# Scores of the sliding-window heads: both groups' products ahead of both minima in their shared bank, and other buffers for the first projection's unsplit input

## The chip, the cores and the metric

The kernel runs on one core of one Trainium2 chip. The time is the device time of one execution in microseconds (us). Before the change it is 308.17 us, the median of 3 runs (307.82 to 308.65).

The core has a matrix engine (TensorE, PE in the profile; its weight loads have a row of their own, PEld), a vector engine (VectorE, DVE), an activation engine (ScalarE, ACT), a small general one (GpSimd, POOL) and one that here only issues transfers (SyncE, SP). Matrix products are accumulated in PSUM, which has banks of 512 fp32 columns for each of 128 partitions; everything else lives in SBUF.

## The reference

One decoder layer on 512 tokens of width 1024, batch 1: a modulated normalisation, one wide projection, two groups of attention heads side by side, a gate on each, an output projection.

```python
mod = jax.nn.silu(c) @ w_ada + b_ada
shift, scale, gate = jnp.split(mod, 3, axis=-1)
h = rms_norm(x, norm_gain) * (1 + scale[:, None, :]) + shift[:, None, :]
proj = h @ w_in
(q_a, k_a, v_a, z_a, q_b, kc, vc, ks, vs, kw, vw, z_b, g_b) = jnp.split(proj, _split_points(), axis=-1)
...
o_a = banded_gqa(qa, ka, heads(v_a, A_KV), SWA_WINDOW, rel_bias[:, :A_HEADS], sinks)
...
o_b = gb[..., 0, :] * o_cmp + gb[..., 1, :] * o_sel + gb[..., 2, :] * o_win
y = jnp.concatenate([o_a.reshape(Bn, S, D_A) * jax.nn.silu(z_a.astype(jnp.float32)),
                     o_b.reshape(Bn, S, D_B) * jax.nn.silu(z_b.astype(jnp.float32))], axis=-1)
out = y.astype(x.dtype) @ w_out
return x + gate[:, None, :] * out
```

Group A has 8 query heads on 2 key/value groups with a window of 128 tokens, a bias by distance and a sink for each head in the softmax. Group B has 8 query heads on 2 groups as well, with a compressed, a selected and a windowed (512) branch.

## The kernel before

**Precision and stages.** The inputs are fp32. A product of two fp32 numbers is made of three products of halves: high by high, high by low and low by high, where high is the number rounded by the engine's fp32r type and low is the rest. So the first projection's input h exists as hh (high), hl (low) and, between the two, hf (unsplit: `h_high`, L285 to L289, writes hh and hf on ScalarE; `h_low`, L291 and L292, subtracts on VectorE). The first projection (queries, keys and values of group A) is an `in_order` section up to 51 us. After it come the other projections (L503, 256 columns each; L513, 512 columns) and, from 65 us on, the attention slots between them. The output projection ends the program.

**Slots.** Attention is cut into slots of 128 queries. A slot of kind a is one query head of each of the two key/value groups (heads r and 4 + r) and one block i of four: 16 slots, from about 65 to 148 us. A slot of kind b does the same for one branch of group B, from about 157 us. `run` (in program order) deals for each step t: the transposes of slot t−2 (`slot_trans`, L971), the scaling of slot t−1 (`slot_scale`, L952 to L960), the scores of slot t (`slot_scores`, L923 to L935), a share of the projections, and after a head's last block the products with the values (`slot_pv`, L998). `block()` keeps TensorE's instructions of these pieces together in this order among each other; between them, and on the other engines, the tile scheduler sets the order from the program order and the buffers in use. A packer gives every pool its places (`auto_bufs`), so another buffer in one place can move tiles in others.

**The scores of a slot.** For each group g two matmuls (by the high and low half of the keys) form 128 by up to 512 products in PSUM; one VectorE instruction (`tensor_tensor_reduce`, L928) adds the bias, writes the sum to P in SBUF and puts the smallest into nm (signs are turned, so it is the softmax maximum). ScalarE takes the exponential (L935) and its sum. In kind a both groups write one bank, `ps_a`, 256 columns each; in kind b each has a bank of its own. The pool of these banks, ps_s, has two.

**Other names.** pt is a bank for transposes, wh and wl the halves of a projection's weights, qs a head's queries, kT the keys, first and rest small constants, gate rows (L248) are VectorE reductions that make the layer's gate from raw rows of weights and lie between group B's slots.

Of the kernel before, what the change touches and what calls it, by code (L numbers as in the profile page):

```python
# [9 lines left out]
F32 = mybir.dt.float32  # L10
# [9 lines left out]
S, D, HD, NB = 512, 1024, 64, 4  # L20
# [62 lines left out]
def hybrid_layer_kernel(ctx, tc, A, out):  # L83
    nc = tc.nc
    PE, DVE, ACT, POOL, SP = nc.tensor, nc.vector, nc.scalar, nc.gpsimd, nc.sync
# [9 lines left out]
    def T2(dt, name):  # L95
        return t2.tile([128, S], dt, name=name, tag="t2")
# [100 lines left out]
    stp = st.enter_context(tc.tile_pool(name="stp", bufs=1))  # L197
# [71 lines left out]
    hf, y, ws = {}, {}, {}  # L269
# [13 lines left out]
            DVE.tensor_tensor(y[k][:, c], xT[k][:, c], by[:, c], op=OP.mult)  # L283

    def h_high(k, parts=(slice(0, S),)):  # L285
        hf[k] = T2(F32, "hf")
        for t in (hh[k], hf[k]):
            for c in (parts if t is hh[k] else parts[:0] + (slice(0, S),)):
                ACT.activation(t[:, c], y[k][:, c], AF.Identity, bias=AB[:, k, 1:2], scale=AB[:, k, 0:1])  # L289
# [16 lines left out]
    with in_order(tc) as begun:  # L306
# [83 lines left out]
        scaled(1, rbp)  # L390
        weights_high(0)
        rb = stp.tile([128, S], F32, name="rb")
        hf[0] = T2(F32, "hf")
        for c in (quarters[0], quarters[1], halves[1]):
            ACT.activation(hh[0][:, c], y[0][:, c], AF.Identity, bias=AB[:, 0, 1:2], scale=AB[:, 0, 0:1])
        ACT.activation(rb, rbp, AF.Copy)
# [8 lines left out]
        def new_tile(k):  # L405

            if k in PE_MOD:
                mod_ab(k)
            h_high(k, halves)
            if k == 7:  # L410
                h_low(k)
                return
            weights_high(k + 1)
            mod_shift(k + 1)
            if k > 1:
                h_low(k)
            mod_scale(k + 1)
            if k == 1:
                h_low(k)
            weights_low(k + 1)  # L420
            if 1 < k < 6:
                scaled(k + 2, rb)
# [56 lines left out]
    ps_s = ctx.enter_context(tc.tile_pool(name="ps_s", bufs=2, space=PSUM))  # L479
# [46 lines left out]
    qs = {}  # L526
    kT = {}
# [360 lines left out]
    def slot_scores_both(sl, P):  # L888

        r = sl["id"][1]  # L890
        nm = sm.tile([128, 2, 2], F32, name="nm2", bufs=2)
        dn = sm.tile([128, 2, 2], F32, name="dn2", bufs=2)
        for g in range(2):
            ps = ps_s.tile([128, 512], F32, name="s")[:, 0:256].rearrange("p (b k) -> p b k", b=2)
            for hl_ in range(2):
                PE.matmul(ps, qs[8 + 4 * g + r][:, 0:128], kTb[g][:, :, hl_, 0:128], start=hl_ == 0, stop=hl_ == 1)
            for b in range(2):
                DVE.tensor_tensor_reduce(out=P[:, g, 128 * b:128 * b + 128], in0=ps[:, b], in1=bias["b", r, g][:, 384:512],
                                         scale=1.0, scalar=3e38, op0=OP.add, op1=OP.min, accum_out=nm[:, g, b:b + 1])
        for g in range(2):  # L900
            for b in range(2):
                v = P[:, g, 128 * b:128 * b + 128]
                ACT.activation(v, v, AF.Exp, bias=nm[:, g, b:b + 1], scale=-1.0, accum_out=dn[:, g, b:b + 1])
        sl.update(P=P, dn=dn, w=256, lo=0)

    def slot_scores(sl):
        kind, r, br, i = sl["id"]
        lo = max(0, i - 1) * 128 if kind == "a" else 0
        w = (i + 1) * 128 - lo
        P = mp.tile([128, 2, 257], F32, name="pa", bufs=3) if kind == "a" else mp.tile([128, 2, 512], F32, name="pp", bufs=3)  # L910
        if br == 3:
            slot_scores_both(sl, P)
            return
        nm = sm.tile([128, 2], F32, name="nm", bufs=4)
        dn = sm.tile([128, 2], F32, name="dn", bufs=4)
        ps_a = ps_s.tile([128, 512], F32, name="s") if kind == "a" else None
        for g in range(2):
            h = (0 if kind == "a" else 8) + 4 * g + r
            n = max(w, 256)
            ps = ps_a[:, 256 * g:256 * g + n] if kind == "a" else ps_s.tile([128, 512], F32, name="s")[:, 0:n]  # L920
            k = kT[br, g]
            for hl_ in range(2):
                PE.matmul(ps, qs[h][:, 128 * i:128 * i + 128], k[:, hl_, lo:lo + n], start=hl_ == 0, stop=hl_ == 1)  # L923
            if kind == "a":
                bt, init = bias["a", r][:, g, 256 - w:256], nsink[:, h:h + 1]
            else:
                bt, init = bias["b", r, g][:, 512 - w:512], 3e38
            DVE.tensor_tensor_reduce(out=P[:, g, 0:w], in0=ps[:, 0:w], in1=bt, scale=1.0, scalar=init,  # L928
                                     op0=OP.add, op1=OP.min, accum_out=nm[:, g:g + 1])
        e = w  # L930
        if kind == "a":
            POOL.tensor_copy(P[:, :, w:w + 1], nsink[:, r:8:4][:, :, None])
            e = w + 1
        for g in range(2):
            ACT.activation(P[:, g, 0:e], P[:, g, 0:e], AF.Exp, bias=nm[:, g:g + 1], scale=-1.0,  # L935
                           accum_out=dn[:, g:g + 1])
        sl.update(P=P, dn=dn, w=w, lo=lo)
# [77 lines left out]
    def run(slots, stream):  # L1015
# [3 lines left out]
        for t in range(n + 3):  # L1019
            per = PER_A if t < 16 else PER_B[t - 16 >= PER_B[2]]  # L1020
            if t < n:
                kind, r, br, i = slots[t]["id"]
                if kind == "a" and i == 0 and r >= 2:
                    load_bias_b(r - 2)
            if 0 <= t - 2 < n:
                with block():
                    slot_trans(slots[t - 2])
            if 0 <= t - 1 < n:
                slot_scale(slots[t - 1])
            if t < n:  # L1030
                with block():
                    slot_scores(slots[t])
            stream.adv(per / 2)
            if 0 <= t - 3 < n:
                group.append(slots[t - 3])
                kind, r, br, i = slots[t - 3]["id"]
                if i == NB - 1 and (kind == "a" or br == 2):
                    with block():
                        for sl in group:
                            slot_pv(sl)  # L1040
                        if jobs:
                            jobs.pop(0)()
                            stream.debt += 3.6
                    group = []
                    if kind == "b" and br == 2 and r + 2 < 4:
                        load_bias_b(r + 2)
            stream.adv(per / 2)
# [103 lines left out]
```

## Time and profile before

| what | us |
|---|---|
| median of 3 runs | 308.17 |
| the profiled execution | 307.14 |
| its span | 305.4 |
| PE busy | 298.1 (98%) |
| DVE busy | 239.0 (78%) |
| ACT busy | 196.3 (64%) |

The profile is of one execution. Its span goes from the first to the last instruction; its time has 1.74 us more around it. Busy times are of the instructions; PE and PEld overlap. A stretch's row ("64.00:85.00 21.00") gives its length and each engine's busy time in it with the number of instructions, then the clock that TensorE was granted, the share of the transfer engines and their rate. A row of the waits reads: engine and line that waited, what it waited for, us in total, times, longest. A row of the timeline reads: start, duration, engine, line, operation, out<-in, and in brackets how long the engine stood idle before it and what ended that.

### The profile page before, as it was taken

The numbers are of one execution on the slowest core, as the hardware profiler recorded it, in microseconds if no ns is written. First come the engines' busy times: TensorE is split into PE (matmuls) and PEld (weight loads), VectorE is DVE, ScalarE is ACT, GpSimd is POOL, SyncE is SP. The second block draws the span as 40 slices with busy tenths as digits, with TensorE's granted clock in tenths as the row PEclk, the third lists the DMA queues.
The fourth block names the chain that finished last, engine by engine and source line by source line (L and its number), as shares of the span: only waits on it lengthen the run. The fifth ranks groups of instructions, "written<-read, shape, count | busy, mean of one in ns | idle before, by whom it ended". The sixth has DMA issues, their size and how long they took to land.

```text
span 305.4 us, 5858 instructions
## 1 busy us (share of the span) xinstructions
PE 298.1 (98%) x2118; PEld 252.6 (83%) x2119; DVE 239.0 (78%) x669; ACT 196.3 (64%) x474; POOL 4.6 (1%) x26
## 2 busy tenths in 40 slices
PE   8899999999999999999999999999999999999995
PEld 4577888888999999999886788788888888788885
DVE  3899996999995487787899999999996985817411
ACT  4876457876885569948657756875876875823200
POOL 1000000100000000000000000000000000000000
PEclk9999999999999999999999999999999999999999
DMA  7999929897233980340542422472000000005401
GB/s 258 384 379 409 386 76 286 293 249 284 75 100 103 345 264 14 102 142 2 170 140 72 138 71 69 131 280 75 21 14 2 0 2 1 2 0 188 158 34 71
DMA packets 27420, 44.21 MB, mean 145 GB/s; under 512 B 1712, under 2 KB 19408, under 8 KB 27392
## 3 DMA queue, kind: packets, MB, share of 16 engines
q1 hardware_dynamic: 27392, 43.84, 41.9%
q8 instruction: 17, 0.28, 0.3%
q14 instruction: 11, 0.09, 0.1%
HBM read 41.70 MB, written 2.14 MB: 144 GB/s over the span
## 4 chain that ended last, share of the span: by engine, by line
PE 79%; DVE 9%; DMA 5%; ACT 3%; issue 2%; SPq 1%; DVEq 0%; ACTq 0%
PE pj L513 29%; PE s L923 8%; PE po L998 8%; PE pj L503 7%; PE sq L299 7%; PE pt L981 4%; PE pt L971 4%; PE skv L300 4%; DMA ada_ring<-in_w_ada_ss 3%; PE s L630 2%; DMA raw<-in_w_cmp 2%; DVE wl L181 2%; DVE qs L563 1%; DVE pa L928 1%; ACT pa L935 1%
## 5 line engine op out<-in xcount | busy, mean ns | idle before, releaser
L180 ACT ACTIVATE wh<-raw 128x512 fp32r<-128x512 f32 (+1 forms) x52 | 31.9, 637 | 18.1 <-PE pj L513 14.0
L181 DVE TENSOR_TENSOR wl<-raw,wh 128x512 fp32r<-128x512 f32 (+1 forms) x52 | 35.4, 689 | 9.3 <-issue 3.4
L503 PE MATMUL pj<-wl,hh 128*128 128x256 f32 (+1 forms) x128 | 36.7, 287 | 0.0
L503 PE MATMUL pj<-wh,hh 128*128 128x256 f32 (+1 forms) x128 | 36.7, 287 | 0.0
L503 PE MATMUL pj<-wh,hl 128*128 128x256 f32 (+1 forms) x128 | 36.5, 285 | 0.0
L935 ACT ACTIVATE pp<-pp,nm 128x256 f32<-128x256 f32 (+2 forms) x48 | 29.2, 610 | 8.8 <-DVE nm L928 8.7
L513 PE MATMUL pj<-hh,wh 128*128 128x512 f32 x80 | 32.3, 403 | 0.0
L513 PE MATMUL pj<-hh,wl 128*128 128x512 f32 x80 | 31.8, 398 | 0.0
L513 PE MATMUL pj<-hl,wh 128*128 128x512 f32 x80 | 31.7, 397 | 0.0
L928 DVE CUSTOM_DVE_ANT_0 pp<-s,bias 128x256 f32<-128x256 f32 (+2 forms) x48 | 25.5, 552 | 2.9 <-PE s L923 2.8
L513 PE MATMUL pj<-yl,wh 128*128 128x512 f32 (+1 forms) x72 | 26.8, 373 | 0.0
L513 PE MATMUL pj<-yh,wl 128*128 128x512 f32 (+1 forms) x72 | 26.8, 372 | 0.0
L513 PE MATMUL pj<-yh,wh 128*128 128x512 f32 (+1 forms) x72 | 26.3, 371 | 0.0
L503 PEld LDWEIGHTS pj<-wl,hh 128*128 128x128 f32 x128 | 24.1, 188 | 0.4 <-issue 0.3
L503 PEld LDWEIGHTS pj<-wh,hh 128*128 128x128 f32 x128 | 24.1, 188 | 0.2 <-issue 0.2
L503 PEld LDWEIGHTS pj<-wh,hl 128*128 128x128 f32 x128 | 24.1, 188 | 0.2 <-issue 0.2
L923 PE MATMUL s<-kTb,qs 128*128 128x256 f32 (+2 forms) x96 | 23.4, 356 | 0.0
L956 DVE TENSOR_SCALAR pp<-pp,rr,grev 128x256 f32<-128x256 f32 (+2 forms) x48 | 21.0, 476 | 0.6
L928 DVE CUSTOM_DVE_ANT_0 pa<-s,bias,nsink 128x256 f32<-128x256 f32 (+1 forms) x32 | 14.3, 449 | 4.9 <-PE s L923 3.4
L982 ACT COPY ptT<-pt 128x384 f32<-128x384 f32 (+1 forms) x32 | 15.7, 527 | 3.6 <-PE pt L981 3.6
L513 PEld LDWEIGHTS pj<-hh,wl 128*128 128x128 f32 x80 | 15.1, 189 | 3.2
L513 PEld LDWEIGHTS pj<-hl,wh 128*128 128x128 f32 x80 | 15.0, 188 | 3.1 <-issue 0.2
(246 smaller groups left out, 702.1 us busy)
## 6 DMA issues: line engine op xcount, KB each, us to landing
ada_ring<-in_w_ada_ss SPq DMA_DIRECT2D x16, 512.0 KB, 9.4
raw<-in_w_cmp SPq DMA_DIRECT2D x8, 512.0 KB, 6.0
raw<-in_w_gate SPq DMA_DIRECT2D x8, 512.0 KB, 3.3
raw<-in_w_o SPq DMA_DIRECT2D x8, 512.0 KB, 5.4
wst_ring<-in_w_qkv_a SPq DMA_DIRECT2D x8, 384.0 KB, 9.2
bias<-line_d SPq DMA_DIRECT2D x8, 256.0 KB, 3.1
xr<-in_xT SPq DMA_DIRECT2D x8, 256.0 KB, 4.1
raw<-in_w_q_b SPq DMA_DIRECT2D x4, 512.0 KB, 5.9
```

The source lines that it names most:

```text
L180: ACT.activation(wh, src, AF.Copy)
L181: DVE.tensor_tensor(wl, src, wh.bitcast(F32), op=OP.subtract)
L299: PE.matmul(pj_q[tb], lt, w[:, 0:512], start=f, stop=l, skip_group_check=True)
L300: PE.matmul(pj_kv[tb // 2][:, tb % 2, :], lt, w[:, 512:768], start=f and tb % 2 == 0, stop=l, skip_group_check=True)
L503: PE.matmul(bank[:, t * n:(t + 1) * n], h[:, tb * 128:(tb + 1) * 128], w[:, k % 2, :], start=k == 0 and m == 0, stop=k == 7 and m == 2)
L513: PE.matmul(bank, w, h[:, cols], start=k == 0 and m == 0, stop=k == 7 and m == 2)
L923: PE.matmul(ps, qs[h][:, 128 * i:128 * i + 128], k[:, hl_, lo:lo + n], start=hl_ == 0, stop=hl_ == 1)
L928: DVE.tensor_tensor_reduce(out=P[:, g, 0:w], in0=ps[:, 0:w], in1=bt, scale=1.0, scalar=init, op0=OP.add, op1=OP.min, accum_out=nm[:, g:g + 1])
L935: ACT.activation(P[:, g, 0:e], P[:, g, 0:e], AF.Exp, bias=nm[:, g:g + 1], scale=-1.0, accum_out=dn[:, g:g + 1])
L956: DVE.tensor_scalar(v, v, rr[:, g:g + 1], gates[:, g, br:br + 1], op0=OP.mult, op1=OP.mult)
L982: ACT.copy(T[:, 0:nb, :], rev(pt[:, 0:nb * 128].rearrange("p (b q) -> p b q", b=nb)))
L998: PE.matmul(o[64 * g:64 * g + 64, 128 * i:128 * i + 128], vb[:, 64 * g:64 * g + 64], sl["T"][g][:, b, :], start=first_of and b == 0, stop= ...
```

## The change

In `slot_scores` the loop over the two groups is split: first all four matmuls, then both minima. In kind a the first group's minimum stood between the two groups' products before. In kind b the code's order changes likewise, each group in its bank. The first projection's unsplit input hf is taken from the stage's pool stp (named hf, two buffers) in place of the general pool t2.

```diff
     def h_high(k, parts=(slice(0, S),)):
-        hf[k] = T2(F32, "hf")
+        hf[k] = stp.tile([128, S], F32, name="hf", bufs=2)
...
         rb = stp.tile([128, S], F32, name="rb")
-        hf[0] = T2(F32, "hf")
+        hf[0] = stp.tile([128, S], F32, name="hf", bufs=2)
...
         ps_a = ps_s.tile([128, 512], F32, name="s") if kind == "a" else None
+        ps = []
         for g in range(2):
             h = (0 if kind == "a" else 8) + 4 * g + r
             n = max(w, 256)
-            ps = ps_a[:, 256 * g:256 * g + n] if kind == "a" else ps_s.tile([128, 512], F32, name="s")[:, 0:n]
-            k = kT[br, g]
+            ps.append(ps_a[:, 256 * g:256 * g + n] if kind == "a" else ps_s.tile([128, 512], F32, name="s")[:, 0:n])
             for hl_ in range(2):
-                PE.matmul(ps, qs[h][:, 128 * i:128 * i + 128], k[:, hl_, lo:lo + n], start=hl_ == 0, stop=hl_ == 1)
+                PE.matmul(ps[g], qs[h][:, 128 * i:128 * i + 128], kT[br, g][:, hl_, lo:lo + n], start=hl_ == 0,
+                          stop=hl_ == 1)
+        for g in range(2):
+            h = (0 if kind == "a" else 8) + 4 * g + r
             if kind == "a":
                 bt, init = bias["a", r][:, g, 256 - w:256], nsink[:, h:h + 1]
             else:
                 bt, init = bias["b", r, g][:, 512 - w:512], 3e38
-            DVE.tensor_tensor_reduce(out=P[:, g, 0:w], in0=ps[:, 0:w], in1=bt, scale=1.0, scalar=init,
+            DVE.tensor_tensor_reduce(out=P[:, g, 0:w], in0=ps[g][:, 0:w], in1=bt, scale=1.0, scalar=init,
                                      op0=OP.add, op1=OP.min, accum_out=nm[:, g:g + 1])
```

From here on the lines of the changed kernel are three higher: the minimum is L931, the exponential L938, the scaling L952 to L963, the transposes L974, the products with the values L1001. The matmuls of the scores stay on L923.

The order of the instructions changes in these places. On TensorE, at slot 13 (about 135 us; kT_645 and kT_647 are the keys of the two groups, qs_921 and qs_924 the queries), before:

```order
L557 MATMUL pt<-first,qn 128x128 x3
L971 MATMUL pt<-first,pa 128x128 [waits PE_49]
L971 MATMUL pt<-first,pa 128x128 x3
L923 MATMUL s<-kT_645,qs_921 128x256 x2
L503 MATMUL pj<-wh,hh 128x256
L503 MATMUL pj<-wl,hh 128x256
L503 MATMUL pj<-wh,hl 128x256
L503 MATMUL pj<-wh,hh 128x256
L503 MATMUL pj<-wl,hh 128x256
L503 MATMUL pj<-wh,hl 128x256
L923 MATMUL s<-kT_647,qs_924 128x256 [waits DVE_49]
```

and now:

```order
L557 MATMUL pt<-first,qn 128x128 x3
L974 MATMUL pt<-first,pa 128x128 [waits PE_49]
L974 MATMUL pt<-first,pa 128x128 x3
L923 MATMUL s<-kT_645,qs_921 128x256 x2
L923 MATMUL s<-kT_647,qs_924 128x256 x2
L503 MATMUL pj<-wl,hh 128x256
L503 MATMUL pj<-wh,hl 128x256
```

The second group's products moved ahead of six projection matmuls and wait for VectorE no more. It is alike in 15 of the 16 slots of group A; in slot 0 the products stay spread out.

On TensorE, at slots 7 and 8 (about 111 us; qs_799 and qs_802 are slot 7's queries, qs_850 and qs_853 slot 8's, gsig the gates of the branches), before:

```order
L923 MATMUL s<-kT_647,qs_802 128x256 [waits DVE_49]
L923 MATMUL s<-kT_647,qs_802 128x256
L971 MATMUL pt<-first,pa 128x128 x4
L923 MATMUL s<-kT_645,qs_850 128x256 x2
L788 MATMUL pt<-gsig,rest 128x96
L503 MATMUL pj<-wh,hh 128x256
L503 MATMUL pj<-wl,hh 128x256
L503 MATMUL pj<-wh,hl 128x256
L923 MATMUL s<-kT_647,qs_853 128x256 [waits DVE_49]
```

and now:

```order
L923 MATMUL s<-kT_645,qs_799 128x256 x2
L923 MATMUL s<-kT_647,qs_802 128x256 x2
L974 MATMUL pt<-first,pa 128x128 x4
L923 MATMUL s<-kT_645,qs_850 128x256 x2
L923 MATMUL s<-kT_647,qs_853 128x256 x2
L788 MATMUL pt<-gsig,rest 128x96 [waits DVE_49]
L503 MATMUL pj<-wh,hl 128x256
```

Slot 7's first products stood six projection matmuls ahead of its second, and now stand right ahead of them; slot 8's second products moved ahead of the gate transpose and three projection matmuls. Slot 7's own transposes come after fourteen projection matmuls in the new order; before they came thirteen after slot 8's second products.

On VectorE, at the first slot of group B (about 160 us; the four L949 rows are its scalings, rr_2105 their factors), before:

```order
L945 RECIPROCAL rr_2105<-dn_2037 128x4
L181 TENSOR_TENSOR wl<-raw,wh 128x512
L861 TENSOR_TENSOR yl_2081<-yf,yh_2080 128x512
L949 TENSOR_SCALAR pp<-pp,rr_2105,grev 128x128 x2
L563 TENSOR_TENSOR qs_2092<-pt,qs_2092 64x512
L949 TENSOR_SCALAR pp<-pp,rr_2105,grev 128x128 x2
L952 RECIPROCAL rr<-dn 128x2
```

and now:

```order
L948 RECIPROCAL rr_2105<-dn_2037 128x4
L248 ISA raw,gate_lsb<-raw,scb,first 128x1024
L248 ISA gate_lsb 128x1
L563 TENSOR_TENSOR qs_2092<-pt,qs_2092 64x512
L181 TENSOR_TENSOR wl<-raw,wh 128x512
L952 TENSOR_SCALAR pp<-pp,rr_2105,grev 128x128
L563 TENSOR_TENSOR qs_2095<-pt,qs_2095 64x512
L952 TENSOR_SCALAR pp<-pp,rr_2105,grev 128x128 x3
```

The gate row, which came ten rows after the last of these scalings, now stands ahead of the first. On TensorE the four transposes of this slot stand ten projection matmuls (L513) later than before.

## The prediction

> **What bounds the kernel now.** I read the engine totals first, then the line of the scores, then the waits stage by stage. The page's first part and the row of group A's minima:
>
> ```profile
> PE 298.1 (98%) x2118; PEld 252.6 (83%) x2119; DVE 239.0 (78%) x669; ACT 196.3 (64%) x474; POOL 4.6 (1%) x26
> ...
> L928 DVE CUSTOM_DVE_ANT_0 pa<-s,bias,nsink 128x256 f32<-128x256 f32 (+1 forms) x32 | 14.3, 449 | 4.9 <-PE s L923 3.4
> ```
>
> TensorE is almost the whole span, so a microsecond in which it stands still is a microsecond of the time, unless a later wait would have stopped it anyway. The query on the scores' line shows where it stands still:
>
> ```profile
> L923 PEld LDWEIGHTS s<-kT,qs x64: 186/189/192, 65.3 to 146.9; 128*128 128x128 f32 x64
> L923 PE MATMUL s<-kT,qs x64: 277/288/388, 65.3 to 147.1; 128*128 128x256 f32 x64
> ...
> its engine sat idle before it (us, times) until:
>   DVE nm L928: 3.9, 14
> ...
> ```
>
> That wait is the second group's products waiting for the first group's minimum, because both write one bank. It is what the change removes: 3.9 us in 14 records. One of them as the timeline has it (start, duration, engine, line; the idle time before and its releaser in brackets), slot 13, TensorE's weight loads:
>
> ```profile
> 135.86 0.19 PEld L503 LDWEIGHTS pj<-wl,hh 128*128 128x128 f32 x1
> 135.98 0.19 PEld L503 LDWEIGHTS pj<-wh,hl 128*128 128x128 f32 x1
> 136.36 0.30 PEld L923 LDWEIGHTS s<-kT,qs 128*128 128x128 f32 x2 [0.19 <-DVE nm L928]
> 136.59 0.19 PEld L503 LDWEIGHTS pj<-wh,hh 128*128 128x128 f32 x1
> ```
>
> Loads follow one another every 0.12 us (135.86 to 135.98), and the one that waited came 0.38 us after its predecessor: 0.26 us lost, which is the bracket's 0.19 and 0.07 more, since a load of 0.19 us normally overlaps the next by 0.07. Per stage the waits of the weight loads are these (total, times, longest), for 64 to 85, 85 to 93, 110 to 121, 121 to 135 and 135 to 148 us in this order:
>
> ```profile
> PEld s L923 <- DVE nm L928: 0.9, 2, 0.5
> PEld s L923 <- DVE nm L928: 0.2, 1, 0.2
> PEld s L923 <- DVE nm L928: 0.6, 3, 0.2
> PEld s L923 <- DVE nm L928: 0.6, 2, 0.4
> PEld s L923 <- DVE nm L928: 0.9, 3, 0.4
> ```
>
> That is 3.2 us in 11 loads. With 0.07 us for each it is 1.04, 0.27, 0.81, 0.74 and 1.11 us: 4.0 us, the most that the change can give through these waits. What each stage lets through depends on the other engines (busy time of PE, PEld, DVE, ACT, POOL in each stretch, granted clock):
>
> ```profile
> 64.00:85.00 21.00, 20.23 (x159) 19.14 (x158) 20.08 (x46) 16.82 (x41) 0.38 (x2) 1.00 0.62 194
> ...
> 110.00:121.00 11.00, 10.98 (x100) 10.06 (x100) 8.92 (x38) 8.79 (x25) 0.77 (x4) 1.00 0.34 114
> 121.00:135.00 14.00, 13.47 (x112) 12.80 (x109) 10.72 (x33) 10.54 (x26) 0.37 (x2) 1.00 0.40 130
> 135.00:148.00 13.00, 12.92 (x111) 11.62 (x110) 9.84 (x25) 11.26 (x28) 0.38 (x2) 1.00 0.07 26
> 148.00:172.00 24.00, 24.00 (x153) 18.16 (x152) 23.36 (x65) 15.52 (x40) 0.00 (x0) 1.00 0.38 125
> ...
> 230.00:272.00 42.00, 42.00 (x383) 35.92 (x379) 28.07 (x94) 27.69 (x77) 0.00 (x0) 1.00 0.01 1
> ```
>
> **The change part by part.** No instruction of the scores is added or removed: the 64 matmuls, 32 minima and 32 exponentials stay. The sum is made against the profiled execution's own 307.14 us (its span of 305.4 and 1.74 around it); the median shown is 308.17, 1.03 more, and the difference I find is taken off that.
>
> *64 to 85 us (slots 0 to 3), 1.04 us removed.* VectorE is busy 20.08 of 21 us here, as nearly full as TensorE, and what follows the scores on TensorE is waiting for VectorE's work. Slot 1's wait and what stands around it:
>
> ```profile
> 73.01 0.48 DVE L928 CUSTOM_DVE_ANT_0 pa<-s,bias,nsink 128x256 f32<-128x256 f32 x1
> 73.42 0.28 DVE L960 TENSOR_SCALAR pa<-pa,rr 128x128 f32<-128x128 f32 x1
> 73.55 0.30 PEld L923 LDWEIGHTS s<-kT,qs 128*128 128x128 f32 x2 [0.43 <-DVE nm L928]
> 73.80 0.24 PEld L971 LDWEIGHTS pt<-first,pa 128*128 128x128 f32 x2
> ```
>
> The transposes that follow at 73.80 need the scaling that ended at 73.70 (73.42 and 0.28). Without the wait at 73.55 TensorE reaches them 0.5 us sooner and waits there for the same scaling. So this stage moves its wait and gains nothing. Bounds: 1.04 gained, or 0.3 lost if slot 0's first minimum, now behind all four products, is late by a gap of VectorE. I take 0.
>
> *85 to 93 us, 0.27 us removed.* One wait, with VectorE no longer full. I take 0.2 (0 to 0.27).
>
> *110 to 121 us (slots 7 to 10), 0.81 us removed.* Here the order of the matmuls packs tighter than the work between allows. Slot 7 in the timeline, from its second products to its transposes:
>
> ```profile
> 111.63 0.30 PEld L923 LDWEIGHTS s<-kT,qs 128*128 128x128 f32 x2 [0.19 <-DVE nm L928]
> 112.17 0.48 DVE L928 CUSTOM_DVE_ANT_0 pa<-s,bias,nsink 128x256 f32<-128x256 f32 x1
> 113.09 0.51 ACT L935 ACTIVATE pa<-pa,nm 128x257 f32<-128x257 f32 x1
> 114.71 1.01 ACT L958 ACTIVATE pa<-pa,rr 128x256 f32<-128x256 f32 x2
> 115.32 0.42 PEld L971 LDWEIGHTS pt<-first,pa 128*128 128x128 f32 x4
> ```
>
> From the second minimum's start to the transposes go 3.15 us (112.17 to 115.32). With all four products together that minimum starts about 1.1 us after the first product's load (four loads at 0.12, 0.28 for the last product and one minimum of 0.41, from 73.01 to 73.42, ahead of it, less overlaps), so the transposes can start some 4.2 us after it, or 3.8 if the later slot's minima are less in the way. By the order TensorE has eight products, four transposes, one gate transpose and fourteen projection matmuls in between: 27 at 0.12, about 3.3 us. A new wait of 0.5 to 1.0 us takes the place of the old ones. I take 0 (0.8 gained to 0.5 lost).
>
> *121 to 135 us (slots 11 and 12), 0.74 us removed.* TensorE has a wait of 0.5 us left on the normalised queries at 133.74, and slot 12's share runs into it; slot 11's does not. I take 0.5 (0 to 0.74).
>
> *135 to 148 us (slots 13 to 15), 1.11 us removed.* VectorE has over 3 us of slack in 13, and the transposes stand well behind the scores (the next load of slot 13 after the products is a projection's). I take 1.0 (0.5 to 1.11).
>
> *148 us on, group B.* Group B's two groups have always had banks of their own, so its products and minima only change their order in the code. TensorE is full here and VectorE nearly so: 23.36 of 24 us. A shift gained before 148 passes through if VectorE comes earlier too, and it stood idle waiting for TensorE's projections just before (9.84 of 13 busy). But the order on VectorE changes: a gate row (L248) stands ahead of the first group-B slot's four scalings, where it stood behind them.
>
> ```profile
> 158.83 0.72 PE L923 MATMUL s<-kTb,qs 128*128 128x256 f32 x4
> 161.73 0.59 DVE L949 TENSOR_SCALAR pp<-pp,rr,grev 128x128 f32<-128x128 f32 x2
> 163.07 0.60 DVE L949 TENSOR_SCALAR pp<-pp,rr,grev 128x128 f32<-128x128 f32 x2
> 163.47 0.33 PE L971 MATMUL pt<-first,pp 128*128 128x128 f32 x1
> 168.02 1.28 DVE L248 CUSTOM_DVE_ANT_0 raw<-raw,scb,first 128x1024 f32<-128x1024 f32 x1
> ```
>
> TensorE already waits for the second pair (released in the middle of the row at 163.07). In the new order 1.28 us of gate row and two rows of some 0.65 stand ahead of the first scaling, 2.6 us; TensorE's transposes come ten projection matmuls later, about 2.3 us by the pitch of the twelve between 158.83 and the first pair of transposes. Nearly even: I take 0.4 us lost (none to 1.3).
>
> *The unsplit input in two buffers of its own.* The eight tiles came one after the other out of the pool t2, in one place; now they have places in another pool. The only thing this frees is ScalarE's write waiting for VectorE's subtraction of the tile before. ScalarE has to wait in the same loop for the scale and shift in any case:
>
> ```profile
> ACT hh L289 <- DVE AB L255: 10.0, 5, 2.2
> ```
>
> Those 10.0 us are the cover; were they gone, ScalarE would still write at the pace of VectorE's subtraction. I take 0. The lower weights' transfers and buffers move around too, because the pools are laid out anew; the order shows no wait added for it.
>
> **Sum.** 0 + 0.2 + 0 + 0.5 + 1.0 − 0.4 = 1.3 us gained: 305.8 us for the profiled execution, **306.9 us** as a median.
>
> **Rivals.**
>
> *All of it is gained.* The slots' later consumers wait nowhere, 4.0 us and no loss in group B: 304.2 us. For it: TensorE is 98% of the span. Against it: the rows at 73.42 and 115.32, where consumers follow directly. The Trainium skill ("Perfetto Trace Analysis", Identifying the Most-Contended Engine) takes the engine of the highest occupancy as the one to work on first; by that rule every wait of TensorE would count, which is this rival, and the stretch from 64 to 85 us, with 20.23 against 20.08 us, disagrees.
>
> *The waits only move.* Stages 121 to 148 behave like the first: queries, keys and transposes stop TensorE at the same times. Then nothing is gained: 308.2 us. For it: each chain through minimum, exponential and scaling is as long as before. Against it: VectorE's 9.84 of 13 us.
>
> *The wait changes sides.* The first minimum now cannot read the shared bank until the second group's two products are in: it waits for two loads more, 2 times 0.12 = 0.23 us. Where VectorE is full (slots 0 to 3) that could cost 4 times 0.23 = 0.9 us of VectorE and so of time: 306.9 + 0.9 = 307.8 us. Against it: VectorE has other rows queued ahead of most minima. The Trainium skill ("PSUM — Partial Sum Buffer", PSUM bank collisions raise a hardware error) has two engines kept apart by bank and quadrant of partitions, not by address, reads against writes in both directions. The row at 136.36 agrees as far as one direction goes: the products went into the other half of the bank and waited. By that rule read in the other direction the sum would be 0.9 us worse in the full stage.
>
> *Slower: the gate row holds up group B.* At 161.7 us the scalings stand behind the gate row's 1.28 us plus its read-out, and TensorE waits for that in full, 1.35 us, with nothing behind to catch it up since VectorE is full until 230 us, and the waits in group A only move, so that nothing was gained before. That gives 308.17 + 1.35 = 309.5 us. It decides when VectorE reaches the row no earlier than before while TensorE has not been put back by the ten matmuls. Against it: those ten.
>
> **How the numbers follow.** Forecast 0.47, all gained 0.12, waits only move 0.23, wait changes sides 0.04, gate row 0.14. What a measurement of this kernel can tell from no change is about 0.3%, 0.92 us: below 307.25 is faster, above 309.09 slower. The forecast's own range comes from its three least certain terms (the first stage up to 1.04 better, 110 to 121 us 0.5 worse, group B 0.9 worse, of which I let one happen at a time): 305.8 to 307.8 us, so a tenth of it lies within 0.3%. Faster: 0.42 + 0.12 = 0.54. Within: 0.05 + 0.23 + 0.04 + 0.01 = 0.33. Slower: 0.13. The range for 8 in 10 leaves out the ends of the full gain and of the gate row: 304.6 to 309.3 us. That takes in the bound of 0.8 more in the stage 110 to 121 and of 1.04 in the first.
>
> **What the changed kernel's profile would show.** The wait of the scores for the minimum in group A gone from 3.9 us to near 0, and in its place waits of the transposes (L974) for the scaling at about 73.7 and 114 us and of the normalised queries at 133 us. If those new waits sum to 4 us, the waits only moved; if they stay under 1 us, all was gained. Slot 15's scores should come about 1.5 us earlier than 146.83, and the end 1.3 us. If minima in group A wait more for TensorE than the 3.4 us they do now, and transposes with them, the wait changed sides. A wait of the transposes near 162 us above 1 us confirms the gate row. The first projection's tiles should show no change. I am wrong if TensorE's projection end moves by under 0.5 us while the scores' waits are gone and no transpose waits.

## The result and the profile after

| kernel | median, us | runs | profiled execution | its span |
|---|---|---|---|---|
| before | 308.25 | 307.82 to 308.65 (6) | 307.14 | 305.4 |
| changed | 306.24 | 306.00 to 307.09 (6) | 306.31 | 304.2 |

The ratio is 0.9938, with a 95% interval of 0.9924 to 0.9952: 0.6% faster. The forecast was 306.9 in a range of 304.6 to 309.3. The two profiled executions differ by only 0.8 us and the medians by 2.0, and that difference turned out to be half of the story.

The engine totals of the changed kernel, from the first part of its page:

```profile
PE 296.2 (97%) x2118; PEld 251.6 (83%) x2119; DVE 238.3 (78%) x669; ACT 195.3 (64%) x474; POOL 3.8 (1%) x26
...
L180 ACT ACTIVATE wh<-raw 128x512 fp32r<-128x512 f32 (+1 forms) x52 | 31.1, 636 | 6.7 <-PE pj L513 4.4
```

The query on the scores' line, as it was read for before:

```profile
L923 PEld LDWEIGHTS s<-kT,qs x64: 186/190/193, 64.6 to 143.8; 128*128 128x128 f32 x64
L923 PE MATMUL s<-kT,qs x64: 277/281/387, 64.7 to 143.9; 128*128 128x256 f32 x64
...
its engine sat idle before it (us, times) until:
  DVE yf L858: 0.3, 1
  ACT kT L581: 0.2, 1
...
who waited for it (us, times):
  DVE pp L931: 3.7, 11
  DVE pa L931: 1.0, 3
```

The wait for the minimum, 3.9 us before, is gone, and group A's minima wait for TensorE 1.0 us where they waited 3.4. So the wait did not change sides in group A; group B's minima wait 3.7 us where they waited 2.8. The last scores of group A start at 143.8 us and not at 146.9: 3.1 us earlier where 1.5 was forecast, in part because slot 15's second products now stand ahead of other matmuls, and 1.2 are left at the end of the span. The waits of TensorE's loads in the changed kernel, by the stages of the prediction (64 to 85, 85 to 93, 110 to 121, 121 to 135, 135 to 148 us, those of 0.2 us left out where larger ones stand):

```profile
PEld pt L974 <- PE pj L503: 0.5, 1, 0.5
PEld pt L974 <- ACT pa L961: 0.4, 1, 0.4
...
PEld pt L576 <- ACT pa L961: 0.3, 1, 0.3
...
PEld pt L974 <- issue: 0.2, 1, 0.2
PEld pt L576 <- issue: 0.2, 1, 0.2
...
PEld pt L557 <- issue: 1.3, 1, 1.3
...
PEld pj L503 <- issue: 0.2, 1, 0.2
```

In the timeline these are four places (the transposes after slots 1 and 3, those of slot 7, the queries of group B):

```profile
73.45 0.20 PEld L974 LDWEIGHTS pt<-first,pa 128*128 128x128 f32 x2 [0.43 <-ACT pa L961]
...
83.54 0.20 PEld L974 LDWEIGHTS pt<-first,pa 128*128 128x128 f32 x2 [0.54 <-PE pj L503]
...
112.38 0.20 PEld L974 LDWEIGHTS pt<-first,pa 128*128 128x128 f32 x2 [0.18 <-issue]
...
132.00 0.42 PEld L557 LDWEIGHTS pt<-first,qn 128*128 128x128 f32 x4 [1.34 <-issue]
```

The first two are the old waits of 0.43 and 0.49 us in a new place, as forecast. The third is small where 0.5 to 1.0 was forecast. The fourth grew from 0.49 to 1.34.

### The profile page after: what moved, and what is told of

It reads as the page before. It is cut to its first block, busy times and chain, and to the rows that moved or that the text cites. A ratio compares the mean times of both kernels' runs of the same rounds, so it can differ in the third digit from the quotient of the medians.

```text
span 304.2 us, 5822 instructions
## 1 busy us (share of the span) xinstructions
PE 296.2 (97%) x2118; PEld 251.6 (83%) x2119; DVE 238.3 (78%) x669; ACT 195.3 (64%) x474; POOL 3.8 (1%) x26
## 4 chain that ended last, share of the span: by engine, by line
PE 74%; DVE 12%; ACT 8%; DMA 3%; issue 2%; SPq 1%; POOL 0%; ACTq 0%; POOLq 0%
PE pj L513 28%; PE sq L299 8%; PE po L1001 8%; PE pj L503 6%; PE s L923 6%; PE skv L300 4%; PE pt L984 4%; PE pt L974 3%; DMA ada_ring<-in_w_ada_ss 3%; PE s L630 2%; ACT pa L938 2%; DVE wl L181 2%; DVE qs L563 1%; ACT wh L180 1%; DVE pa L931 1%
## 5 line engine op out<-in xcount | busy, mean ns | idle before, releaser
L180 ACT ACTIVATE wh<-raw 128x512 fp32r<-128x512 f32 (+1 forms) x52 | 31.1, 636 | 6.7 <-PE pj L513 4.4
L938 ACT ACTIVATE pp<-pp,nm 128x256 f32<-128x256 f32 (+2 forms) x48 | 29.3, 612 | 7.8 <-DVE nm L931 7.7
L513 PE MATMUL pj<-hh,wl 128*128 128x512 f32 x80 | 32.3, 404 | 0.0
L513 PE MATMUL pj<-hh,wh 128*128 128x512 f32 x80 | 32.1, 401 | 0.0
L513 PE MATMUL pj<-hl,wh 128*128 128x512 f32 x80 | 31.7, 396 | 0.0
L931 DVE CUSTOM_DVE_ANT_0 pp<-s,bias 128x256 f32<-128x256 f32 (+2 forms) x48 | 25.6, 552 | 4.0 <-PE s L923 3.7
L513 PE MATMUL pj<-yh,wl 128*128 128x512 f32 (+1 forms) x72 | 26.8, 373 | 0.0
L513 PE MATMUL pj<-yl,wh 128*128 128x512 f32 (+1 forms) x72 | 26.7, 371 | 0.0
L513 PE MATMUL pj<-yh,wh 128*128 128x512 f32 (+1 forms) x72 | 26.4, 371 | 0.0
L923 PE MATMUL s<-kTb,qs 128*128 128x256 f32 (+2 forms) x96 | 23.7, 359 | 0.0
L1080 DVE SCALAR_TENSOR_TENSOR fin<-pj,gate_lsb,xr 128x512 f32<-128x512 f32 (+1 forms) x9 | 6.2, 690 | 16.1 <-PE pj L513 16.1
L513 PEld LDWEIGHTS pj<-hl,wh 128*128 128x128 f32 x80 | 15.0, 188 | 3.2
L513 PEld LDWEIGHTS pj<-hh,wl 128*128 128x128 f32 x80 | 15.1, 189 | 2.9
```

Of the source, the lines that this page charges most:

```text
L180: ACT.activation(wh, src, AF.Copy)
L513: PE.matmul(bank, w, h[:, cols], start=k == 0 and m == 0, stop=k == 7 and m == 2)
L923: PE.matmul(ps[g], qs[h][:, 128 * i:128 * i + 128], kT[br, g][:, hl_, lo:lo + n], start=hl_ == 0, stop=hl_ == 1)
L931: DVE.tensor_tensor_reduce(out=P[:, g, 0:w], in0=ps[g][:, 0:w], in1=bt, scale=1.0, scalar=init, op0=OP.add, op1=OP.min, accum_out=nm[:, g: ...
```

## Half of the gain comes from somewhere else

The second profile of the kernel before (before_again, below) has a span of 306.6 us, 1.2 more than the first. The whole difference lies at one place. SyncE's issues of the small constants and the first weights in this second profile, and ScalarE and TensorE behind them:

```profile
42.90 0.33 SPq L429 DMA_DIRECT2D rest<-in_rest  x1
43.32 3.13 SPq L161 DMA_DIRECT2D raw<-in_w_kv_cmp  x2
...
50.09 0.60 ACT L466 ACTIVATE qsq<-sq 128x512 f32<-128x512 f32 x1 [0.86 <-PE sq L299]
52.01 1.68 ACT L180 ACTIVATE wh<-raw 128x512 fp32r<-128x512 f32 x3 [1.33 <-DMA raw<-in_w_kv_cmp]
...
62.86 0.20 PEld L576 LDWEIGHTS pt<-first,kn 128*128 128x128 f32 x2 [1.37 <-DVE kn L571]
```

The same issues in the first profile of before, and ScalarE at the same place:

```profile
43.06 0.33 SPq L429 DMA_DIRECT2D rest<-in_rest  x1
43.49 3.13 SPq L161 DMA_DIRECT2D raw<-in_w_kv_cmp  x2
...
50.81 1.68 ACT L180 ACTIVATE wh<-raw 128x512 fp32r<-128x512 f32 x3
```

And in the changed kernel:

```profile
35.93 0.33 SPq L429 DMA_DIRECT2D rest<-in_rest  x1
36.35 9.94 SPq L161 DMA_DIRECT2D raw<-in_w_kv_cmp  x2
...
50.47 1.66 ACT L180 ACTIVATE wh<-raw 128x512 fp32r<-128x512 f32 x3
```

In the kernel before, the load of the small constants waits at the head of SyncE's queue until 43 us, because its place in SBUF still holds a tile that VectorE reads (L283). The first weights (kv_cmp) stand behind it. They land about when ScalarE wants to split them, in one execution in time, in another 1.3 us late; behind the split, in ScalarE's order, wait the squares (L466) for the norms, then VectorE's norms, then the keys' first transposes. Twelve executions of before have spans from 304.9 to 306.8 us. In the changed kernel the constants have a place that is free, SyncE goes on at 36 us, and six executions have spans from 304.1 to 304.3.

In the order of SyncE's instructions this is one word, before and after:

```
L429 DMA rest<-in_rest 128x960 [waits DMAHW1_49,DVE_49]
L429 DMA rest<-in_rest 128x960 [waits DMAHW1_49]
```

## The experiments

To compare kernels whose orders differ I use TensorE's **stall so far**: the start of a weight load in the trace, less the time that all loads ahead of it take at their usual pitch (0.12 us at 256 columns, 0.23 at 512, 0.11 at a transpose, 0.11 for each product with the values). All kernels do the same matmuls, so the differences of it between two places say where time was lost, wherever the order has put the work. The places are 54 us of work (about 61 us in the trace, the first projection done), 148 us of work (about 165 us in before, group B's first slot) and 276 us (the end).

| kernel | median, us | span | up to 54 | 54 to 148 | 148 to 276 |
|---|---|---|---|---|---|
| before, first profile | 308.25 | 305.4 | 7.6 | 9.6 | 5.3 |
| before_again | 308.18 | 306.6 | 8.8 | 9.6 | 5.3 |
| changed | 306.24 | 304.2 | 7.4 | 7.6 | 6.4 |
| hf_only | 307.96 | 306.9 | 9.1 | 9.7 | 5.3 |
| first_head_only | 308.12 | 306.2 | 8.5 | 9.7 | 5.3 |
| two_banks | 306.11 | 304.7 | 8.2 | 7.2 | 6.3 |
| rest_later | 307.21 | 305.4 | 7.3 | 9.9 | 5.3 |
| late_slots_rest_later | 307.18 | 305.1 | 7.3 | 8.8 | 6.2 |
| two_banks_rest_later | 305.73 | 303.7 | 7.5 | 7.4 | 6.0 |
| changed_rest_later | 305.98 | 304.0 | 7.4 | 7.7 | 6.1 |
| all_but_slot14 | 306.47 | 304.2 | 6.9 | 8.3 | 6.1 |
| all_but_slot15 | 305.06 | 302.8 | 6.8 | 7.9 | 5.3 |

The first four of the experiments ran together (before on that chip: 307.93), the next four (308.41) and the last two (307.72). So medians are compared within a group; from one group to another the ratios to before are.

**before_again**: no edit.

> The kernel before, unchanged, for a second profile. My theory: the profiled execution of before (307.14 us, span 305.4) lay about 1 us under its own median, because the time around the span or the span varies from run to run; a second profile then gives a span of 305.4 to 306.4 us and the timed runs are at 308.2. The rival, that the profiled span is the rule and only the time around the span differs (2.1 in the kernel after, 1.7 before): span 305.4 again and timed runs at 307.5 to 308.2 with the rest outside the span.

Measured: ratio 1.0004 (0.9989 to 1.0018), span 306.6, the timed runs with spans from 304.9 to 306.8. The span itself varies, so the first profile was one of the lucky executions.

**hf_only**: the first half of the change alone.

```diff
-        hf[k] = T2(F32, "hf")
+        hf[k] = stp.tile([128, S], F32, name="hf", bufs=2)
```

> Only the unsplit input gets its own buffers; the scores stay as before. Every engine has the same instructions in the same order as before. My theory: no difference, within 0.2 us of before, and no wait of the first projection or of the weights' splitting changes by over 0.1 us. The rival, that the new places are worth the 0.26 us by which the changed kernel is ahead at the end of the first projection (61.38 against 61.65 us): 0.2 to 0.3 us faster, with TensorE at 61.4 us at the first keys' transposes.

Measured: 307.96 us, ratio 1.001 (0.9997 to 1.0023). No difference. In its profile the weights were late again (ScalarE's split waits 1.53 us for them), so the new places of this tile alone do not free the constants' place; the layout of both edits together does. With the new buffers and the new order in slots 0 to 3 alone (first_head_only) the constants still wait until 42.44 us. No run has the new order in all slots without the new buffers, so what the order alone would do to the layout is not shown.

**two_banks**: before with a bank for each group.

```diff
-        ps_a = ps_s.tile([128, 512], F32, name="s") if kind == "a" else None
...
-            ps = ps_a[:, 256 * g:256 * g + n] if kind == "a" else ps_s.tile([128, 512], F32, name="s")[:, 0:n]
+            ps = ps_s.tile([128, 512], F32, name="s")[:, 0:n]
```

> Before, but in group A each of the two groups gets a bank of its own from the same pool of two; the code's order (products, minimum, products, minimum) stays. My theory, that the shared bank alone makes the second products wait: the wait of the group-A scores for the minimum falls from 3.9 us to under 0.5, the products stand next to each other on TensorE, and the time falls by 1 to 2.5 us, as in the changed kernel. The rival, that the order of the code matters and banks do not, because VectorE is what paces the slots: the wait stays or moves to the next slot's first products (both banks now are in use between slots), and the time stays within 0.7 us of before.

Measured: 306.11 us, ratio 0.9942 (0.9920 to 0.9963). What TensorE waits for at group A's scores in it (the scores stand on L922 there):

```profile
its engine sat idle before it (us, times) until:
  ACT kT L581: 0.9, 3
```

The minimum is no longer there, with the code in the old order. The bank that both groups share is the cause of the wait; splitting the loop and splitting the bank take it away alike. The bank is one tile there, and this edit splits both, so whether the wait is set by the bank or by the tile no run tells apart.

**first_head_only**: the changed kernel, the new order in slots 0 to 3 alone.

```diff
+            if kind == "b" or r > 0:
+                minimum(g, h)
+        for g in range(2):
...
+            if not (kind == "b" or r > 0):
+                minimum(g, h)
```

(`minimum` holds the bias, the first value and the reduction as they stand in the code.)

> The changed kernel, but the new order of the scores only in the first head pair's slots (0 to 3, 64 to 85 us); slots 4 to 15 are as before. My theory, that VectorE is full there and the removed 1.0 us turns up ahead of the transposes: TensorE gains 0 to 0.4 us by 85 us, and the time is within 0.5 us of before. The rival, that every wait of TensorE counts: 1.0 us gained by 85 us and 1.0 us faster.

Measured: 308.12 us, ratio 1.0008 (0.9996 to 1.0020). From 54 to 74 us of work, which are the first four slots, its stall is 2.70 us, and 2.68 in before_again. The full stage gives nothing, as forecast: the transposes after slot 1 wait for the scaling (L974 of the changed kernel is L981 here, the scaling L968):

```profile
74.97 0.20 PEld L981 LDWEIGHTS pt<-first,pa 128*128 128x128 f32 x2 [0.42 <-ACT pa L968]
75.14 0.54 PEld L932 LDWEIGHTS s<-kT,qs 128*128 128x128 f32 x4
```

**rest_later**: before with the load of the constants behind the first weights.

```diff
             if k == LW - 1:
+                for _ in range(2):
+                    load_next()
                 SP.dma_start(rest[:, 0:960], A["rest"])
-                for _ in range(5):
+                for _ in range(3):
                     load_next()
```

> Before, with one line moved: the load of the small constants (rest) is issued behind the first two weight loads (kv_cmp) and no longer ahead of them on SyncE's queue. In the kernel before that load waits until 43 us for a place in SBUF and holds up the weights behind it; in the changed kernel the new layout takes this wait away and the first weights start at 36 us. My theory: this is the part of the gain that I had not foreseen. The first weights start near 36 us, ScalarE does not wait for them at 50 us, the keys' first transposes are at 61.4 to 61.8 us in every execution and not at 62.9, and the median is 306.7 to 307.2 us, 0.8 to 1.3 under before, with a spread under 0.8 us. The rival, that the late weights only lie beside another wait: within 0.4 us of before.

Measured: 307.21 us (307.01 to 307.36), ratio 0.9964 (0.9951 to 0.9977), 1.2 us under before, and a spread of 0.35 us. SyncE and ScalarE in it:

```profile
36.37 6.98 SPq L161 DMA_DIRECT2D raw<-in_w_kv_cmp  x2
45.82 0.34 SPq L431 DMA_DIRECT2D rest<-in_rest  x1
...
47.73 2.18 ACT L180 ACTIVATE wh<-raw 128x512 fp32r<-128x512 f32 x4
49.99 1.58 ACT L468 ACTIVATE qsq<-sq 128x512 f32<-128x512 f32 x3
```

ScalarE has split all four pieces before the squares. The stall up to 54 us of work is 7.3 us, as in the changed kernel. The keys' first transposes even come at 59.8 us, earlier than expected, because the scheduler puts fewer projection matmuls ahead of them.

**late_slots_rest_later**: rest_later with the new order of the scores in slots 8 to 15.

```diff
+            if kind == "b" or r < 2:
+                minimum(g, h)
```

> The same line moved, the unsplit input where it was before, and the new order of the scores only in slots 8 to 15. Against rest_later this shows what the later half of the slots is worth. My theory: the waits removed there are 2.0 us, the queries' transposes at 132 us take 0.5 to 0.8 back, group B takes 0.3 to 1.0 back: 0.4 to 1.0 us under rest_later, 305.9 to 306.6. The rival, that the gain comes from slots 4 to 7, where I had forecast none: within 0.3 us of rest_later.

Measured: 307.18 us (306.75 to 308.85), ratio 0.9971 (0.9956 to 0.9986), against 307.21: a miss, though the profiled span is 0.3 us shorter. The stall up to 148 us of work falls by 1.1, as it should, and group B's rises from 5.3 to 6.2. The rival's number came, and with it part of its reason: against changed_rest_later (below), which has the new order in all slots and the same order in group B, this kernel has 1.1 us more stall from 54 to 148 us of work, and its median is 1.2 us higher. So the new order in slots 0 to 7 is worth as much as in slots 8 to 15. As first_head_only finds nothing for slots 0 to 3 alone, this comes with slots 4 to 7. TensorE and VectorE have in group B the order of the changed kernel here, whatever arrives there. That gave the question of the last two runs.

**two_banks_rest_later**:

> Two banks in group A and the line moved, the scores in the old order of the code. The profile of two_banks had the late weights (1.3 us) and a span of 304.7. My theory: the two gains are independent and add up: 1.0 to 1.4 us under two_banks, 304.8 to 305.2 us, faster than the changed kernel by 1 us. The rival, that what is gained ahead of 65 us is lost in the full stages after it: 305.8 to 306.2, like two_banks.

Measured: 305.73 us (305.49 to 305.98), ratio 0.9917 (0.9899 to 0.9936). Faster than two_banks, by 0.4 us where 1.0 to 1.4 was expected; but the two ran on different chips, and each against before on its own chip the gains are 2.7 and 1.8 us, 0.9 apart. Of two_banks' six executions, with spans from 303.3 to 305.1, the profiled one (304.7) had late weights (1.31 us); that the shorter ones had not is likely, and no trace shows it. In the table all the difference in the span is up to 54 us and in group B. Beside changed_rest_later, of the same group, a bank for each group does at least as well as the new order (305.73 against 305.98 us).

**changed_rest_later**: the changed kernel with the same line moved.

> The changed kernel with the same line moved. My theory: the changed kernel has the early weights already, so nothing is left: 306.0 to 306.5 us. The rival, that the gain of the early weights in rest_later is from something else that the line moves: 0.5 us or more under the changed kernel.

Measured: 305.98 us (305.88 to 306.50), ratio 0.9930 (0.9912 to 0.9947), spans of 304.0 to 304.1: next to nothing left to gain, so the changed kernel has the early weights. Against rest_later, with the weights early in both, the scores' order is worth 307.21 − 305.98 = 1.2 us (the two differ in the unsplit input's buffers as well, which alone made no difference).

**all_but_slot15** and **all_but_slot14**: changed_rest_later with one slot in the old order.

```diff
+            if kind == "b" or 4 * r + i == 15:
+                minimum(g, h)
```

> changed_rest_later, but slot 15 keeps the old order of its scores. With that the scheduler deals group B's instructions on TensorE and VectorE exactly as in the kernel before, while group A's other fifteen slots stand as in the changed kernel. My theory: what group A gains passes through group B whole, and the 0.8 us that the changed kernel loses there (span from the end of group A on, against before) is the price of group B's new order alone. Slot 15's wait costs about 0.3 us, the old order gives 0.8 back: 0.4 to 0.6 us under changed_rest_later, 305.4 to 305.6 us, and the path from 148 us of work to the end takes 5.3 us of stalls as before and not 6.1. The rival, that VectorE is full in group B and swallows part of any gain: no faster than changed_rest_later, 306.0 to 306.5.

> The control: slot 14 keeps the old order in place of slot 15. Group B's order stays that of the changed kernel, and only slot 14's second products move. My theory: slot 14's wait of 0.36 us comes back and nothing else: 306.2 to 306.5 us, with 6.1 us of stalls from 148 us of work on. The rival (a slot's wait lies beside another wait): 306.0 as changed_rest_later.

Measured: all_but_slot15 305.06 us (304.71 to 305.36), ratio 0.9914 (0.9899 to 0.9930); all_but_slot14 306.47 (306.00 to 307.08), ratio 0.9962 (0.9948 to 0.9975). The two differ by 1.4 us in the median and by 1.0 in the median of their spans, and both have one slot in the old order; what differs besides is group B's order. In the table 0.4 us of the difference lies ahead of 148 us of work and 0.8 behind it. With the old order of group B TensorE's stall from 148 us of work on is 5.3 us, as in before, rest_later and first_head_only, whose stall up to there is 14.7 us in the one and 17.2 to 18.2 in the others. With the new one it is 6.1, as in changed_rest_later and late_slots_rest_later (6.2); in the changed kernel it is 6.4. So group B passes on whatever it is given, and its new order costs 0.8 us (1.1 in the first profiles). By the ratios all_but_slot15 is 0.5 us under changed_rest_later, as expected. By the medians it is 0.9, of which 0.6 arise ahead of 54 us of work and are no work of slot 15: all_but_slot14, of the same group, has them too. By the ratios it is 0.7 us under the changed kernel (0.9914 and 0.9938), and level with two_banks_rest_later (0.9917).

Where the order costs: the gate row that the prediction names, and the scalings behind it, in the changed kernel:

```profile
159.95 1.25 DVE L248 CUSTOM_DVE_ANT_0 raw<-raw,scb,first 128x1024 f32<-128x1024 f32 x1
...
162.57 0.34 DVE L952 TENSOR_SCALAR pp<-pp,rr,grev 128x128 f32<-128x128 f32 x1
...
163.66 0.86 DVE L952 TENSOR_SCALAR pp<-pp,rr,grev 128x128 f32<-128x128 f32 x3
...
163.03 0.14 PEld L974 LDWEIGHTS pt<-first,pp 128*128 128x128 f32 x1 [0.39 <-issue]
164.06 0.14 PEld L974 LDWEIGHTS pt<-first,pp 128*128 128x128 f32 x1 [0.43 <-DVE pp L952]
```

and the same transposes and the gate row in all_but_slot15 (L983 and L248):

```profile
159.62 0.33 PEld L983 LDWEIGHTS pt<-first,pp 128*128 128x128 f32 x2 [0.29 <-issue]
160.91 0.14 PEld L983 LDWEIGHTS pt<-first,pp 128*128 128x128 f32 x1 [0.28 <-DVE pp L961]
...
165.46 1.28 DVE L248 CUSTOM_DVE_ANT_0 raw<-raw,scb,first 128x1024 f32<-128x1024 f32 x1
```

The transposes wait 0.82 us against 0.57: 0.25 of the 0.8 us at most is the gate row's. By the stall so far another 0.5 arises between 185 and 215 us of work (2.0 us in changed_rest_later, 1.5 in all_but_slot15). Which of the moved instructions cause it stays open.

## Why the prediction was right, and where it was not

*The sign and the size of the scores' part: right, the size in part by luck.* Forecast 1.3 us, measured 1.2 between rest_later and changed_rest_later. The terms are off against each other: group A gained 2.0 to 2.2 us in the table (54 to 148) where 1.7 was forecast, and group B lost 0.8 to 1.1 where 0.4 was. In this list the stall is taken between the same two instructions of both kernels, so that no wait falls on the other side of an edge; the first pair is before and the changed kernel, the second, with the early weights, is rest_later and changed_rest_later.

- *64 to 85 us, forecast 0, and 85 to 93 us, forecast 0.2.* Too small. For slots 0 to 3 alone first_head_only shows 0.0: the wait went to the transposes, at the places named. But from 54 us of work to the transpose of the compressed keys (L683, at 109.92 us in before and 108.39 in the changed kernel) the stall falls by 0.8 us in the first pair and 0.5 in the second. In late_slots_rest_later, with slots 0 to 7 in the old order, it is that of rest_later. Part of the 0.8 is not the minimum's: between 64 and 85 us the scores' waits for the keys' copies (L581 and L582) fall from 0.7 to 0.4 us. What makes up the rest is open.
- *110 to 121 us, forecast 0, and 121 to 135 us, forecast 0.5.* From that transpose to the queries' transposes (133.74 and 132.00 us) the stall falls by 0.5 us in the first pair and 1.0 in the second. The sum is near the forecast, the way to it is not. "A new wait of 0.5 to 1.0 us takes the place of the old ones" was the step that failed: the row at 112.38 has 0.18. I had taken the 3.15 us from the second minimum to the transposes as a chain that would stay. In the changed kernel it is 2.31 us (110.07 to 112.38):

```profile
110.07 0.48 DVE L931 CUSTOM_DVE_ANT_0 pa<-s,bias,nsink 128x256 f32<-128x256 f32 x1
...
111.91 0.35 DVE L963 TENSOR_SCALAR pa<-pa,rr 128x256 f32<-128x256 f32 x1
...
111.97 0.50 ACT L961 ACTIVATE pa<-pa,rr 128x256 f32<-128x256 f32 x1
```

In before slot 8's second exponential (114.31 us on ScalarE) and a row of the keys' norm (L569, 114.27 us on VectorE) ran ahead of slot 7's scaling; in the changed kernel they come behind it (112.37 and 112.77 us). In the other direction the queries' wait grew from 0.49 to 1.34 us, which the term of 0.5 had not allowed for. That the two errors cancel in the first pair is luck.

- *135 to 148 us, forecast 1.0.* From the queries' transposes to the last scores the stall falls by 0.9 us in both pairs. Right. Behind them the next queries' transposes (about 153 us) wait 0.6 us where they waited 0.2.
- *Group B, forecast 0.4 lost.* The sign was right and the mechanism half: 0.8 to 1.1 lost, of which the gate row makes 0.25 at most. The new order costs more at later places that I had not looked at.

*The unsplit input: right for itself, wrong as a sentence about its surroundings.* hf_only shows no difference. But "the order shows no wait added for it" looked for added waits only. One was taken away, that of the constants' load on SyncE, and with it 1.2 us by the medians of before and rest_later. No term of the sum held this; without it the forecast's 1.3 us would have been the whole. That the 2.0 us measured still lie within the range is luck, since nothing in the range stood for it.

*The step that hid it* was the first: the sum was made against a profiled execution that lay 1.03 us under the median, and I passed this on as an offset. By before_again and rest_later that 1.03 us was the late weights, which the profiled execution happened not to have. The range held because it was wider than the 0.7 us that were missing.

*The rivals.* All gained: no, the waits of 1.34, 0.54 and 0.43 us in the rows above took their part. Waits only move: true of slots 0 to 3 by themselves, and in part of the queries at 132 us. Wait changes sides: no, the waits of group A's minima for the products fell from 3.4 to 1.0 us. The Trainium skill's rule of keeping engines apart by bank ("PSUM — Partial Sum Buffer", PSUM bank collisions raise a hardware error) fits the old wait, which is gone in two_banks (0 of 3.9 us left), and read in the other direction it cost nothing here. Gate row: real, at a fifth of the price given or less. On the Trainium skill's rule of the highest occupancy ("Perfetto Trace Analysis", Identifying the Most-Contended Engine): the trace agrees with it for group A after 85 us and for group B, where 7.9 to 9.9 us of stall in group A changed nothing of group B's 5.3 in its old order, though VectorE is busy 23.36 of 24 us at its start. It does not hold in the stretch from 64 to 85 us, where the waits that were taken away came back.

## What to carry to other kernels

Where the profiled execution lies clear under the median of the runs, take a second profile before any sum: the difference is a wait that this execution did not have. Read the queues of transfers for waits that a change takes away, also where it only moves a buffer: a new layout can free the head of a queue, and this was worth as much here as the change to the scores. And where a scheduler sets the order, one slot written in another way can shift the order of a later stage; here that was worth 0.8 us, and the kernel with one slot left in the old order is the faster one. A bank for each group takes the same wait away and leaves the order of the loop as it was.

## What was not expected of the hardware

The same two transfers, issued at the same time after the start (43.32 and 43.49 us), were ready in one execution when ScalarE came to them at 50.81 and in another only at 52.01 us. Why is open. Twelve executions of before spread over 1.9 us of span. With the transfers issued at 36 us the spans spread over 0.1 to 0.4 us in four kernels, over 0.7 in the last two, and over 1.4 in late_slots_rest_later, where one execution of twelve stands alone by 0.9. How much of each spread the landing makes is seen only in the profiled executions: the wait for these transfers at ScalarE's second piece was 0 and 1.33 us in the two of before, 1.53 in hf_only, 1.47 in first_head_only and 1.31 in two_banks.
